# Start addresses of the matmul operands: spare bytes in the slots of the split weights, and a shift of 64 bytes for part of them

## The chip, the cores and the metric

The kernel runs on one core of a Trainium2 chip. The metric is the device time of one execution in microseconds, and smaller is better. Before the change the median of three runs is 1490.11 us (1489.65 to 1490.30). On-chip memory (SBUF) has 128 partitions; a tile of shape `[128, n]` in float32 takes `4 n` bytes at the same byte address in every partition, and "address" below means that byte address. TensorE (PE) multiplies a stationary operand, which a weight load (PEld) puts into the array, with a moving operand, which it streams column by column out of SBUF; the results are added up in PSUM.

## The reference

One layer of a decoder block over 256 tokens of width 2048, in float32: an RMS norm, one wide projection `w_in` (2048 x 11264), three branches (S5 scan, RG-LRU, stick-breaking attention), their gated merge, `w_out`, a residual, a second norm and a squared-ReLU MLP with `w_up` (2048 x 8192) and `w_down` (8192 x 2048), and a last norm.

```
xn = rms_norm(h, norm_mix_g)
proj = xn @ w_in                 # u_s5, u_lru, q, k, v, then 3 x 2048 gate logits
merged = g_s5 * (y_s5 @ w_br_s5) + g_lru * (y_lru @ w_br_lru) + g_attn * (y_attn @ w_br_attn)
h = h + merged @ w_out
hn = rms_norm(h, norm_mlp_g)
h = h + relu(hn @ w_up)**2 @ w_down
return rms_norm(h, final_norm_g)
```

Nearly all the work is in the matrix products with the eight weight matrices.

## The kernel before

**Split operands.** Each float32 matrix product is done as three products of a narrower type (float32r, four bytes in memory): an operand is split into a high part and a low part, and the product is high x high + high x low + low x high.

**The stream of weights.** All weight matrices are cut into units of 256 rows by 512 columns, 128 partitions x 2 x 512 numbers, 4096 bytes a partition. One list, `stream`, orders all 521 units. A unit is loaded into one of three `raw` slots by a DMA from SyncE (L130). ScalarE (ACT) rounds it into a `hi` slot (L146), VectorE (DVE) subtracts to fill a `lo` slot (L147); there are four slots of each, used in turn. `next_unit` keeps four units loaded and three split ahead of TensorE.

**Two forms of a chunk.** A chunk is 512 columns of a weight matrix against all its rows. Both forms compute three matmuls for each piece and differ in what is stationary:

- `chunk` (L225 to L227, tiles `mm_...`), the 256-column form: 128 columns of the weights are stationary, the 256 tokens are moving. The order is: weights `hi` with moving `xhi`, weights `hi` with moving `xlo`, weights `lo` with moving `xhi`. It serves eight chunks of `w_in` (numbers 0 to 7: u_s5, u_lru, q, k) and the two chunks of `w_glu`. There the high and low halves of the moving operand are `xhi`, `xlo` (for `w_glu`: `yg_hi`, `yg_lo`).
- `chunk_tok` (L241 to L243, tiles `mt_...`) and `pair_tok` (L276 to L278, tiles `mp_...`), the 512-column form: 128 tokens are stationary, 512 weight columns are moving. The order is: `xhi` with moving `hi`, `xhi` with moving `lo`, `xlo` with moving `hi`. It serves everything else; the tokens' halves are then `xhi`/`xlo`, `hhi`/`hlo`, or the `yhi`/`ylo` buffers (`ylru_`, `ya_`, `ys_`, `mg_`, `hd_`).

The branches' own work (scans, attention, transposes) is cut into small steps that `pump` issues between units of the stream; their few matmuls (`ps_...`) stand between those of the chunks. They are plain float32, but for `ps_v` (L665), which is float32r with 96 rows. TensorE executes all matmuls in the order in which they are written.

**Which two operands are read at one time.** The weight load of the next matmul is issued while the present matmul streams its moving operand. So in the 256-column form the pairs (moving now, stationary loaded for the next) are `xhi`/`hi`, `xlo`/`lo`, `xhi`/`hi`; in the 512-column form they are `hi`/`xhi`, `lo`/`xlo`, `hi`/`xhi`.

**Where the operands lie.** Pools are laid out one behind the other, and every slice that a matmul reads starts a multiple of 512 bytes into its slot. All sizes of slots are multiples of 512 too, so that in the built program all these slices, `hi`, `lo`, `xhi`, `xlo`, `yhi` and `ylo` alike, start at 32 modulo 512: in both forms, both operands of a pair start at the same address modulo 512. Among the small matmuls' operands, `tri` and `ones` (stationary for `ps_c`), `wrwi`, `stk`, and the attention tiles start at 160 modulo 256, that is 128 further on.

Of the kernel before, what the change touches and what calls it, by code (L numbers as in the profile page):

```python
# [9 lines left out]
F32 = mybir.dt.float32  # L10
F32R = mybir.dt.float32r
# [3 lines left out]
P = 128  # L15
L = 256
D = 2048
KT = D // P
CH = 512
UK = 2  # L20
W = 1024
WT = W // P
NG = 64
NT = 4
# [14 lines left out]
GELU_K = 0.044715  # L39


def units_of(k, n):
    return (n // CH) * (k // (P * UK))

# [2 lines left out]
def hybrid_block(ctx: ExitStack, tc: tile.TileContext, io, out):  # L47
# [2 lines left out]

    const = ctx.enter_context(tc.tile_pool(name="const", bufs=1))
    wraw = ctx.enter_context(tc.tile_pool(name="wraw", bufs=3))
    whi = ctx.enter_context(tc.tile_pool(name="whi", bufs=4))
    act = ctx.enter_context(tc.tile_pool(name="act", bufs=1))
    ypool = ctx.enter_context(tc.tile_pool(name="ypool", bufs=2))
    tmp = ctx.enter_context(tc.tile_pool(name="tmp", bufs=2))
    psm = ctx.enter_context(tc.tile_pool(name="psm", bufs=4, space=PSUM))
    pss = ctx.enter_context(tc.tile_pool(name="pss", bufs=4, space=PSUM))
# [2 lines left out]
    stream = []  # L61
# [36 lines left out]
    for q in range(NQ):  # L98
# [5 lines left out]
        for c in range(2, 4):  # L104
            stream.extend(("w_down", c, q * (FQ // (P * UK)) + g) for g in range(FQ // (P * UK)))
    ngrp = {"w_in": D, "w_br_lru": W, "w_br_attn": W, "w_br_s5": W, "w_glu": W,
            "w_out": D, "w_up": D, "w_down": DFF}

    raw, hi, anchor = {}, {}, {}
    st = {"load": 0, "split": 0, "use": 0}  # L110

    def pieces(i):
        return [slice(k, k + 1) for k in range(UK)] if i == 0 else [slice(0, UK)]
# [19 lines left out]
    def split_next():  # L133
        i = st["split"]
        if i >= len(stream):
            return
        st["split"] += 1
        h = whi.tile([P, UK, CH], F32R, tag="hi", name=f"hi{i}")
        l_ = whi.tile([P, UK, CH], F32R, tag="lo", name=f"lo{i}")
        r = raw.pop(i)  # L140
        x = anchor.pop("x", None)
        es = ExitStack()
        if i == 0:
            es.enter_context(tc.issue_after(x))
        for k in pieces(i):
            anchor["act"] = nc.scalar.copy(h[:, k, :], r[:, k, :]).ins  # L146
            anchor["dve"] = nc.vector.tensor_tensor(l_[:, k, :], r[:, k, :], h[:, k, :].bitcast(F32), ALU.subtract).ins  # L147
        es.close()
        hi[i] = h, l_
# [143 lines left out]

    tc.keep_in_program_order(nc.scalar.preload_act_table_set("natural_log_exp_and_others"))
    gm = small("norm_mix_g")
    xT = act.tile([P, KT, L], F32, tag="m16", name="xT")
    xhi = act.tile([P, KT, L], F32R, tag="xhi", name="xhi")
    xlo = act.tile([P, KT, L], F32R, tag="xlo", name="xlo")
    load_x(0)
    for q in range(3):  # L300
        load_next()
# [30 lines left out]
    nc.gpsimd.affine_select(keep, ones, pattern=[[1, P]], compare_op=ALU.is_gt, fill=0.0, base=0, channel_multiplier=-1)  # L332
    drop = const.tile([P, P], F32, name="drop")
    nc.gpsimd.tensor_scalar(drop, keep, 1e30, -1e30, ALU.mult, ALU.add)
    eps_t = const.tile([P, 1], F32, name="eps_t")
    nc.gpsimd.memset(eps_t, EPS)
    half_pi = const.tile([P, 1], F32, name="half_pi")
    nc.gpsimd.memset(half_pi, math.pi / 2)
    magic = const.tile([P, 1], F32, name="magic")
    nc.gpsimd.memset(magic, MAGIC)  # L340

    def rsqrt_mean(o, ps, n):
# [4 lines left out]
        nc.vector.scalar_tensor_tensor(o, t, 1.5, r, ALU.add, ALU.mult)  # L347

    rstd = const.tile([P, L], F32, name="rstd")
    rstd_tok = const.tile([P, 2], F32, name="rstd_tok")  # L350

    def norm1():
        yield
# [131 lines left out]
    br_ = small("lru_b_r")  # L485
    bi_ = small("lru_b_i")
    lam = small("lru_lambda")
    sp4 = const.tile([P, WT], F32, name="sp4")
    nsp8 = const.tile([P, WT], F32, name="nsp8")
    tiny = const.tile([P, 1], F32, name="tiny")  # L490
    nc.gpsimd.memset(tiny, 2.0 ** -115)
    wrwi = sp.tile([P, 2, WT, P], F32, tag="stk", name="wrwi")
    wr, wi = wrwi[:, 0], wrwi[:, 1]
# [9 lines left out]
    def lru_params():  # L503
        for _ in range(4):
            yield
        lc = const.tile([P, 4, WT], F32, name="lc")
        nc.vector.scalar_tensor_tensor(lc[:, 0, :], lam, -1.0, lam, ALU.mult, ALU.min)
        nc.scalar.activation(lc[:, 1, :], lc[:, 0, :], AF.Exp)
        nc.scalar.activation(lc[:, 2, :], lc[:, 1, :], AF.Ln, bias=1.0)
        nc.vector.tensor_scalar(lc[:, 3, :], lam, -1.0, 0.0, ALU.mult, ALU.max)  # L510
        nc.vector.tensor_tensor(lc[:, 3, :], lc[:, 3, :], lc[:, 2, :], ALU.add)
        nc.vector.tensor_scalar(sp4, lc[:, 3, :], 4.0, None, ALU.mult)
        nc.vector.tensor_scalar(nsp8, lc[:, 3, :], -8.0, None, ALU.mult)
        yield
        yield from lru_load()

    ylru_hi = ypool.tile([P, WT, L], F32R, tag="yhi", name="ylru_hi")
    ylru_lo = ypool.tile([P, WT, L], F32R, tag="ylo", name="ylru_lo")

    def lru_half(c, us):  # L520
        parts = []
# [111 lines left out]
    gq = []  # L633

    def s5_scan():
        v = ypool.tile([P, 2, NT, L], F32, tag="yhi", name="s5_v")
        t12 = ypool.tile([P, 2, NT, L], F32, tag="ylo", name="s5_t")
        vr, vi, t1, t2 = v[:, 0], v[:, 1], t12[:, 0], t12[:, 1]
        tabs, more = s5_tables(0)
        yield from more  # L640
# [18 lines left out]
        for b in range(WT):  # L659
            c, s = tabs  # L660
# [31 lines left out]
            for x_ in (t1, t3):  # L692
                for t in range(NT):
                    j = b * NT + t
# [47 lines left out]
            if n % step == step - 1:  # L742
                yield

    merged = act.tile([P, KT, L], F32, tag="m16", name="merged")
    m_tok = merged.rearrange("p k l -> p (k l)").rearrange("p (t c) -> p t c", t=2)

    def gates(idx, c, alloc):
# [39 lines left out]

    at = ExitStack()
    ap_ = at.enter_context(tc.tile_pool(name="attn", bufs=1))  # L790
    ya_hi = ypool.tile([P, WT, L], F32R, tag="yhi", name="ya_hi")
    ya_lo = ypool.tile([P, WT, L], F32R, tag="ylo", name="ya_lo")
    Z = 384

    def diag(t):
# [84 lines left out]
        finish(t)  # L880


    yg_hi = ypool.tile([P, WT, L], F32R, tag="yhi", name="yg_hi")
    yg_lo = ypool.tile([P, WT, L], F32R, tag="ylo", name="yg_lo")
    for q in range(4):
        s = slice(2 * q, 2 * q + 2)
        nc.scalar.activation(yg_hi[:, s, :], us5[:, s, :], AF.Copy, scale=0.5)
        nc.vector.scalar_tensor_tensor(yg_lo[:, s, :], us5[:, s, :], 0.5, yg_hi[:, s, :].bitcast(F32), ALU.mult, ALU.subtract)
    ys_hi = ypool.tile([P, WT, L], F32R, tag="yhi", name="ys_hi")
    ys_lo = ypool.tile([P, WT, L], F32R, tag="ylo", name="ys_lo")  # L890
    for c in range(2):
        banks = chunk("w_glu", c, W, lambda kt: (yg_hi[:, kt, :], yg_lo[:, kt, :]))
        for j in range(2):
            g = tmp.tile([P, 2, L], F32, tag="gate", name=f"glu_{c}_{j}", bufs=3)
            for h in range(2):
                k = c * 4 + 2 * j + h
# [6 lines left out]
    mg = [None, None]  # L903

    def split_pair(i, n, src):
        if mg[i // 8] is None:
            mg[i // 8] = tuple(ypool.tile([P, WT, L], F32R, tag=t, name=f"mg_{t}{i}") for t in ("yhi", "ylo"))
# [13 lines left out]
    for a in S5_TAIL:  # L921
        c = int(a[1])
# [24 lines left out]
    hT = act.tile([P, KT, L], F32, tag="m16", name="hT")  # L947
    hhi = act.tile([P, KT, L], F32R, tag="xhi", name="hhi")
    hlo = act.tile([P, KT, L], F32R, tag="xlo", name="hlo")
    h_tok = mlp.tile([P, 2, D], F32, name="h_tok")  # L950

    def ms(kt):
# [22 lines left out]
                yield  # L975
        return gen

    rs2 = const.tile([P, 2], F32, name="rs2")
    rq, rfl = [deque(), 2.0, 0.0], {}

    def out_done(c, banks):
# [85 lines left out]
    for q in range(NQ):  # L1067
        hd, hf = {}, {}

        def up_done(cu, banks):  # L1070
            c = cu % (FQ // CH)
            if c % 2 == 0:
                hd[c // 2] = (ypool.tile([P, WT, L], F32R, tag="yhi", name=f"hd_hi{q}_{c}"),
                              ypool.tile([P, WT, L], F32R, tag="ylo", name=f"hd_lo{q}_{c}"))
# [106 lines left out]
```

## Time and profile before

| What | Value |
|---|---|
| Median of three runs | 1490.11 us (1489.65 to 1490.30) |
| The profiled execution's own time | 1491.41 us |
| Its span, first to last instruction | 1489.7 us |
| TensorE busy | 1478.5 us (99%) |
| VectorE busy | 1175.7 us (79%) |
| ScalarE busy | 775.4 us (52%) |
| DMA | 62.5% of 16 engines on the weights' queue |
| Matmuls of the 256-column form | 1728, mean 283 to 287 ns each |
| Matmuls of the 512-column form | 389 ns each |

Matmuls are pipelined: a row's duration runs from a matmul's start to its modelled end, and the next one starts before that. So the pace of TensorE is not in the mean duration but in the distance from one start to the next, which the timeline shows to 0.01 us, and which a count over a window shows more finely. All times in windows are from the start of the span.

### The profile page before, as it was taken

What the parts mean: (1) busy time and instruction counts of PE and PEld (TensorE: products, weight loads), DVE (VectorE), ACT (ScalarE), POOL (GpSimd) and SP (SyncE); (2) the same over time, 40 slices, a digit from 0 to 9 for tenths busy, and PEclk for the clock granted to TensorE, in tenths of its full rate; (3) what the DMA queues carried; (4) which work ended last, traced back from release to release, by engine and by line L of the source; (5) the groups of instructions that cost most, each with busy time, mean ns of one, the idle gap of its engine ahead of it and who ended that gap; (6) DMA issues with size and microseconds to landing.
All of it is one profiled execution on the core that took longest, in us unless ns stands there. A gap on an engine that the chain in (4) does not pass through costs nothing.

```text
span 1489.7 us, 19903 instructions
## 1 busy us (share of the span) xinstructions
PE 1478.5 (99%) x7518; PEld 1259.3 (85%) x7518; DVE 1175.7 (79%) x1470; ACT 775.4 (52%) x915; POOL 48.4 (3%) x73
## 2 busy tenths in 40 slices
PE   9999999999999999999999999999999999999997
PEld 9998888989888888888888888888888888888886
DVE  6878999887989998789799896568754886458955
ACT  6767556565765564544454544344433453344443
POOL 1400000000000000000000000000000000000010
PEclk9999999999999999999999999999999999999999
DMA  9557776655556756566856657666666566666664
GB/s 274 189 157 216 209 229 208 184 165 188 170 177 199 224 184 210 188 187 210 268 183 189 195 184 222 189 193 188 200 194 196 187 197 197 192 190 196 189 198 137
DMA packets 89570, 292.41 MB, mean 196 GB/s; under 512 B 12802, under 2 KB 17026, under 8 KB 89346
## 3 DMA queue, kind: packets, MB, share of 16 engines
q1 hardware_dynamic: 89042, 290.55, 62.5%
q8 instruction: 59, 0.97, 0.3%
q10 hardware_dynamic: 432, 0.59, 0.1%
q14 instruction: 37, 0.30, 0.1%
HBM read 282.71 MB, written 2.10 MB: 191 GB/s over the span
## 4 chain that ended last, share of the span: by engine, by line
PE 95%; DVE 2%; ACT 1%; DMA 1%; issue 1%; DVEq 0%; ACTq 0%; SPq 0%
PE mt_w_in L241 7%; PE mt_w_in L243 7%; PE mt_w_in L242 7%; PE mt_w_up L241 7%; PE mt_w_up L243 7%; PE mt_w_up L242 7%; PE mp_w_down L278 4%; PE mp_w_down L277 4%; PE mp_w_down L276 4%; PE mt_w_down L242 4%; PE mt_w_down L241 4%; PE mt_w_down L243 4%; PE mm_w_in L225 3%; PE mm_w_in L227 3%; PE mm_w_in L226 3%; PE mt_w_br_attn L241 1%
## 5 line engine op out<-in xcount | busy, mean ns | idle before, releaser
L146 ACT CAST hi<-raw 128x1024 fp32r<-128x1024 f32 (+1 forms) x521 | 545.2, 1050 | 614.2 <-PE mt_w_up L243 116.8
L147 DVE TENSOR_TENSOR lo<-raw,hi 128x1024 fp32r<-128x1024 f32 (+1 forms) x521 | 637.1, 1224 | 276.2 <-ACT hi L146 268.5
L241 PE MATMUL mt_w_in<-hi,xhi 128*128 128x512 f32 x448 | 176.2, 393 | 0.0
L243 PE MATMUL mt_w_in<-hi,xlo 128*128 128x512 f32 x448 | 174.5, 389 | 0.0
L242 PE MATMUL mt_w_in<-lo,xhi 128*128 128x512 f32 x448 | 174.4, 389 | 0.0
L241 PE MATMUL mt_w_up<-hi,hhi 128*128 128x512 f32 x448 | 174.3, 389 | 0.0
L242 PE MATMUL mt_w_up<-lo,hhi 128*128 128x512 f32 x448 | 174.3, 389 | 0.0
L243 PE MATMUL mt_w_up<-hi,hlo 128*128 128x512 f32 x448 | 174.3, 389 | 0.0
L225 PE MATMUL mm_w_in<-xhi,hi 128*128 128x256 f32 x512 | 146.7, 287 | 0.7 <-ACT hi L146 0.7
L227 PE MATMUL mm_w_in<-xhi,lo 128*128 128x256 f32 x512 | 145.6, 285 | 1.4 <-DVE lo L147 1.4
L226 PE MATMUL mm_w_in<-xlo,hi 128*128 128x256 f32 x512 | 145.6, 285 | 0.0
L741 DVE STREAM_TRANSPOSE reluT<-relu 32x256 f32<-32x256 f32 x256 | 111.5, 436 | 4.2
L242 PE MATMUL mt_w_down<-lo,hd_hi 128*128 128x512 f32 (+1 forms) x272 | 102.5, 377 | 0.0
L241 PE MATMUL mt_w_down<-hi,hd_hi 128*128 128x512 f32 (+1 forms) x272 | 102.4, 377 | 0.0
L243 PE MATMUL mt_w_down<-hi,hd_lo 128*128 128x512 f32 (+1 forms) x272 | 102.4, 376 | 0.0
L225 PEld LDWEIGHTS mm_w_in<-xhi,hi 128*128 128x128 f32 x512 | 99.1, 194 | 1.9 <-ACT hi L146 1.0
L227 PEld LDWEIGHTS mm_w_in<-xhi,lo 128*128 128x128 f32 x512 | 98.8, 193 | 1.9 <-DVE lo L147 1.8
L276 PE MATMUL mp_w_down<-hi,hd_hi 128*128 128x512 f32 x256 | 99.6, 389 | 0.0
L277 PE MATMUL mp_w_down<-lo,hd_hi 128*128 128x512 f32 x256 | 99.6, 389 | 0.0
L278 PE MATMUL mp_w_down<-hi,hd_lo 128*128 128x512 f32 x256 | 99.6, 389 | 0.0
L226 PEld LDWEIGHTS mm_w_in<-xlo,hi 128*128 128x128 f32 x512 | 99.2, 194 | 0.1
L243 PEld LDWEIGHTS mt_w_in<-hi,xlo 128*128 128x128 f32 x448 | 84.1, 188 | 17.7
(294 smaller groups left out, 2358.1 us busy)
## 6 DMA issues: line engine op xcount, KB each, us to landing
raw<-in_w_in SPq DMA_DIRECT2D x175, 512.0 KB, 4.2
raw<-in_w_up SPq DMA_DIRECT2D x128, 512.0 KB, 4.3
raw<-in_w_down SPq DMA_DIRECT2D x128, 512.0 KB, 4.2
raw<-in_w_out SPq DMA_DIRECT2D x32, 512.0 KB, 4.4
raw<-in_w_br_lru SPq DMA_DIRECT2D x16, 512.0 KB, 4.6
raw<-in_w_br_attn SPq DMA_DIRECT2D x16, 512.0 KB, 4.3
raw<-in_w_br_s SPq DMA_DIRECT2D x16, 512.0 KB, 4.3
stk<-ux SPq DMA_DIRECT2D x96, 64.0 KB, 4.3
```

Source lines behind the costliest of these rows:

```text
L146: anchor["act"] = nc.scalar.copy(h[:, k, :], r[:, k, :]).ins
L147: anchor["dve"] = nc.vector.tensor_tensor(l_[:, k, :], r[:, k, :], h[:, k, :].bitcast(F32), ALU.subtract).ins
L225: nc.tensor.matmul(o, wh[:, kk, s], xh, start=first and ct % 2 == 0, stop=False, skip_group_check=True)
L226: nc.tensor.matmul(o, wh[:, kk, s], xl, start=False, stop=False, skip_group_check=True)
L227: mm = nc.tensor.matmul(o, wl[:, kk, s], xh, start=False, stop=last and ct % 2 == 1, skip_group_check=True)
L241: nc.tensor.matmul(banks[j], xh[:, s], wh[:, a:b], start=kt == 0, stop=False)
L242: nc.tensor.matmul(banks[j], xh[:, s], wl[:, a:b], start=False, stop=False)
L243: return nc.tensor.matmul(banks[j], xl[:, s], wh[:, a:b], start=False, stop=kt == ng * UK - 1)
L276: nc.tensor.matmul(o, xh[:, s], wh[:, kk, :], start=kt == 0, stop=False)
L277: nc.tensor.matmul(o, xh[:, s], wl[:, kk, :], start=False, stop=False)
L278: mm = nc.tensor.matmul(o, xl[:, s], wh[:, kk, :], start=False, stop=kt == ng * UK - 1)
L741: nc.vector.transpose(d_[32 * a:32 * a + 32, :, :, 32 * b:32 * b + 32], s_[32 * b:32 * b + 32, :, :, 32 * a:32 * a + 32])
```

## The change

No instruction is added, removed or moved: on every engine the built program has the same instructions in the same order with the same waits as before. What changes is where tiles lie.

- Each `hi` and `lo` slot is 4160 bytes, 64 more than the unit needs. The slots stand in the order hi0, lo0, hi1, lo1, hi2, lo2, hi3, and lo3 in a pool of its own. Between slots there are 128 bytes of small constants that used to lie in the `const` pool (`lc`, `sp4`, `eps_t` and so on), so that each pair of slots starts 8448 = 33 x 256 bytes after the last.
- The high halves of the tokens (`xhi`, `hhi`, `yhi`) lie in a pool ahead of these slots, the low halves (`xlo`, `hlo`, `ylo`) in one behind them.
- `shift` gives 16 elements, 64 bytes, for units of the 256-column form (`w_glu`, and `w_in` with chunk numbers under 8) and 0 for all others; the split writes the unit that much further into its slot, and the matmuls read it there.

Start addresses in the built programs:

| Operand | Before, modulo 256 | After, modulo 256 |
|---|---|---|
| `xhi`, `hhi`, `yhi` | 32 | 160 |
| `xlo`, `hlo`, `ylo` | 32 | 224 |
| `hi`, 512-column form | 32 | 160 |
| `lo`, 512-column form | 32 | 224 |
| `hi`, 256-column form | 32 | 224 |
| `lo`, 256-column form | 32 | 32 |
| `raw` | 32 | 160 |
| `stk`, `wrwi`, attention tiles, `tri`, `ones` | 160 | 160 |

So the stationary slice of a pair starts, modulo 256, 0 bytes after the moving one in both forms before the change; after it, 0 in the 512-column form and 64 in the 256-column form. Modulo 512 the slots are not alike after the change: `hi` starts at 160 in slots 0 and 2 and at 416 in slots 1 and 3, `lo` at 224 in slots 0 and 2 and at 480 in slots 1 and 3, while the tokens' halves start at 160 and 480.

```diff
+SLOTS = 4
+SHIFT = 16
+
+def shift(name, c, g):
+    return SHIFT if name == "w_glu" or name == "w_in" and c < 8 else 0
...
-    whi = ctx.enter_context(tc.tile_pool(name="whi", bufs=4))
-    act = ctx.enter_context(tc.tile_pool(name="act", bufs=1))
-    ypool = ctx.enter_context(tc.tile_pool(name="ypool", bufs=2))
+    wide = ctx.enter_context(tc.tile_pool(name="wide", bufs=1))
+    act_hi = ctx.enter_context(tc.tile_pool(name="act_hi", bufs=1))
+    wsplit = ctx.enter_context(tc.tile_pool(name="wsplit", bufs=1))
+    act_lo = ctx.enter_context(tc.tile_pool(name="act_lo", bufs=1))
+    wlast = ctx.enter_context(tc.tile_pool(name="wlast", bufs=1))
...
+    def slot(i):
+        j = i % SLOTS
+        pools = wsplit, wlast if j == SLOTS - 1 else wsplit
+        return [p_.tile([P, UK * CH + SHIFT], F32R, tag=f"{n}{j}", name=f"{n}{i}") for p_, n in zip(pools, ("hi", "lo"))]
+
+    def row(name, n):
+        return wsplit.tile([P, n], F32, name=name)
+
+    first = [slot(0)]
+    lc = row("lc", 4 * WT).rearrange("p (a k) -> p a k", a=4)
+    first.append(slot(1))
+    sp4, nsp8, rstd_tok, eps_t = row("sp4", WT), row("nsp8", WT), row("rstd_tok", 2), row("eps_t", 1)
+    first.append(slot(2))
+    half_pi, magic, tiny, rs2 = row("half_pi", 1), row("magic", 1), row("tiny", 1), row("rs2", 2)
+    first.append(slot(3))
...
-        h = whi.tile([P, UK, CH], F32R, tag="hi", name=f"hi{i}")
-        l_ = whi.tile([P, UK, CH], F32R, tag="lo", name=f"lo{i}")
+        o = shift(*stream[i])
+        h, l_ = (t[:, o:o + UK * CH].rearrange("p (k c) -> p k c", k=UK) for t in (first[i] if i < SLOTS else slot(i)))
...
-    xT = act.tile([P, KT, L], F32, tag="m16", name="xT")
-    xhi = act.tile([P, KT, L], F32R, tag="xhi", name="xhi")
-    xlo = act.tile([P, KT, L], F32R, tag="xlo", name="xlo")
+    xT = wide.tile([P, KT, L], F32, tag="m16", name="xT")
+    xhi = act_hi.tile([P, KT, L], F32R, tag="xhi", name="xhi")
+    xlo = act_lo.tile([P, KT, L], F32R, tag="xlo", name="xlo")
...
-    ylru_hi = ypool.tile([P, WT, L], F32R, tag="yhi", name="ylru_hi")
-    ylru_lo = ypool.tile([P, WT, L], F32R, tag="ylo", name="ylru_lo")
+    ylru_hi = act_hi.tile([P, WT, L], F32R, tag="yhi", name="ylru_hi", bufs=2)
+    ylru_lo = act_lo.tile([P, WT, L], F32R, tag="ylo", name="ylru_lo", bufs=2)
```

The other tiles of the old `act` and `ypool` pools move to `wide`, `act_hi` and `act_lo` in the same way.

More of the change, by code (lines that the diff above doesn't have):

```diff
@@ L334, in hybrid_block @@
     nc.gpsimd.tensor_scalar(drop, keep, 1e30, -1e30, ALU.mult, ALU.add)
-    eps_t = const.tile([P, 1], F32, name="eps_t")
     nc.gpsimd.memset(eps_t, EPS)
-    half_pi = const.tile([P, 1], F32, name="half_pi")
     nc.gpsimd.memset(half_pi, math.pi / 2)
-    magic = const.tile([P, 1], F32, name="magic")
     nc.gpsimd.memset(magic, MAGIC)
@@ L349, in hybrid_block @@
     rstd = const.tile([P, L], F32, name="rstd")
-    rstd_tok = const.tile([P, 2], F32, name="rstd_tok")
     def norm1():
@@ L487, in hybrid_block @@
     lam = small("lru_lambda")
-    sp4 = const.tile([P, WT], F32, name="sp4")
-    nsp8 = const.tile([P, WT], F32, name="nsp8")
-    tiny = const.tile([P, 1], F32, name="tiny")
     nc.gpsimd.memset(tiny, 2.0 ** -115)
@@ L505, in lru_params @@
             yield
-        lc = const.tile([P, 4, WT], F32, name="lc")
         nc.vector.scalar_tensor_tensor(lc[:, 0, :], lam, -1.0, lam, ALU.mult, ALU.min)
@@ L635, in s5_scan @@
     def s5_scan():
-        v = ypool.tile([P, 2, NT, L], F32, tag="yhi", name="s5_v")
-        t12 = ypool.tile([P, 2, NT, L], F32, tag="ylo", name="s5_t")
+        v = act_hi.tile([P, 2, NT, L], F32, tag="yhi", name="s5_v", bufs=2)
+        t12 = act_lo.tile([P, 2, NT, L], F32, tag="ylo", name="s5_t", bufs=2)
         vr, vi, t1, t2 = v[:, 0], v[:, 1], t12[:, 0], t12[:, 1]
@@ L743, in blocks @@
                 yield
-    merged = act.tile([P, KT, L], F32, tag="m16", name="merged")
+    merged = wide.tile([P, KT, L], F32, tag="m16", name="merged")
     m_tok = merged.rearrange("p k l -> p (k l)").rearrange("p (t c) -> p t c", t=2)
@@ L790, in hybrid_block @@
     ap_ = at.enter_context(tc.tile_pool(name="attn", bufs=1))
-    ya_hi = ypool.tile([P, WT, L], F32R, tag="yhi", name="ya_hi")
-    ya_lo = ypool.tile([P, WT, L], F32R, tag="ylo", name="ya_lo")
+    ya_hi = act_hi.tile([P, WT, L], F32R, tag="yhi", name="ya_hi", bufs=2)
+    ya_lo = act_lo.tile([P, WT, L], F32R, tag="ylo", name="ya_lo", bufs=2)
     Z = 384
@@ L880, in hybrid_block @@
         finish(t)
-    yg_hi = ypool.tile([P, WT, L], F32R, tag="yhi", name="yg_hi")
-    yg_lo = ypool.tile([P, WT, L], F32R, tag="ylo", name="yg_lo")
+    yg_hi = act_hi.tile([P, WT, L], F32R, tag="yhi", name="yg_hi", bufs=2)
+    yg_lo = act_lo.tile([P, WT, L], F32R, tag="ylo", name="yg_lo", bufs=2)
     for q in range(4):
@@ L888, in hybrid_block @@
         nc.vector.scalar_tensor_tensor(yg_lo[:, s, :], us5[:, s, :], 0.5, yg_hi[:, s, :].bitcast(F32), ALU.mult, ALU.subtract)
-    ys_hi = ypool.tile([P, WT, L], F32R, tag="yhi", name="ys_hi")
-    ys_lo = ypool.tile([P, WT, L], F32R, tag="ylo", name="ys_lo")
+    ys_hi = act_hi.tile([P, WT, L], F32R, tag="yhi", name="ys_hi", bufs=2)
+    ys_lo = act_lo.tile([P, WT, L], F32R, tag="ylo", name="ys_lo", bufs=2)
     for c in range(2):
@@ L906, in split_pair @@
         if mg[i // 8] is None:
-            mg[i // 8] = tuple(ypool.tile([P, WT, L], F32R, tag=t, name=f"mg_{t}{i}") for t in ("yhi", "ylo"))
+            mg[i // 8] = tuple(p_.tile([P, WT, L], F32R, tag=t, name=f"mg_{t}{i}", bufs=2) for p_, t in ((act_hi, "yhi"), (act_lo, "ylo")))
         h_, l_ = mg[i // 8]
@@ L946, in hybrid_block @@
     mf.append(chained(mq, split_tok(3, mlp.tile([P, 4, L], F32, tag="reluT", name="mT3", bufs=2))))
-    hT = act.tile([P, KT, L], F32, tag="m16", name="hT")
-    hhi = act.tile([P, KT, L], F32R, tag="xhi", name="hhi")
-    hlo = act.tile([P, KT, L], F32R, tag="xlo", name="hlo")
+    hT = wide.tile([P, KT, L], F32, tag="m16", name="hT")
+    hhi = act_hi.tile([P, KT, L], F32R, tag="xhi", name="hhi")
+    hlo = act_lo.tile([P, KT, L], F32R, tag="xlo", name="hlo")
     h_tok = mlp.tile([P, 2, D], F32, name="h_tok")
@@ L976, in residual @@
         return gen
-    rs2 = const.tile([P, 2], F32, name="rs2")
     rq, rfl = [deque(), 2.0, 0.0], {}
@@ L1072, in up_done @@
             if c % 2 == 0:
-                hd[c // 2] = (ypool.tile([P, WT, L], F32R, tag="yhi", name=f"hd_hi{q}_{c}"),
-                              ypool.tile([P, WT, L], F32R, tag="ylo", name=f"hd_lo{q}_{c}"))
+                hd[c // 2] = (act_hi.tile([P, WT, L], F32R, tag="yhi", name=f"hd_hi{q}_{c}", bufs=2),
+                              act_lo.tile([P, WT, L], F32R, tag="ylo", name=f"hd_lo{q}_{c}", bufs=2))
             h_, l_ = hd[c // 2]
```

## The prediction

> **What bounds the kernel now.** I read the page's first two parts, then who waits for whom, then TensorE's groups, then single stretches of its timeline.
>
> ```profile
> span 1489.7 us, 19903 instructions
> PE 1478.5 (99%) x7518; PEld 1259.3 (85%) x7518; DVE 1175.7 (79%) x1470; ACT 775.4 (52%) x915; POOL 48.4 (3%) x73
> PE mm_w_in L227 <- DVE lo L147: 1.4, 1, 1.4
> PE warm L327 <- POOL eps_t L336: 1.0, 1, 1.0
> PE mm_w_in L225 <- ACT hi L146: 0.7, 1, 0.7
> ```
>
> The last three rows are all of TensorE's waits: 3.1 us, in the first microseconds. From then on it always has a matmul to start, so the time is the sum of the distances between starts, and a change that moves no instruction can act on it only through these distances, or by making ACT or DVE so late that waits appear. Two groups carry the sum:
>
> ```profile
> L225 PE MATMUL mm_w_in<-xhi,hi 128*128 128x256 f32 x512 | 146.7, 287 | 0.7 <-ACT hi L146 0.7
> L225 PE MATMUL mm_w_glu<-yg_hi,hi 128*128 128x256 f32 x64 | 18.2, 285 | 0.0
> L146 ACT CAST hi<-raw 128x1024 fp32r<-128x1024 f32 (+1 forms) x521 | 545.2, 1050 | 614.2 <-PE mt_w_up L243 116.8
> 587.00:609.00 22.00, 22.00 (x186) 1.00 0.62 193
> 820.00:1460.00 640.00, 640.00 (x2826) 1.00 0.62 195
> ```
>
> The 256-column form has three matmuls of each kind: 3 x (512 + 64) = 1728. Its units are 72 (each gives 24 matmuls); the cast's 521, less one for the first unit, which comes in two pieces, leaves 448 units of 12 matmuls, about 5,380 of the 512-column form. The last two rows are windows with TensorE alone (time, busy, matmuls, granted clock, DMA share, GB/s). Matmuls that only reach into a window at its ends are counted too, about two, so a start comes every 22.0/184 = 0.120 us in the first (256 columns) and every 640/2824 = 0.2266 us in the second (512). The timeline shows the 256-column pace row by row, and the passage to the other form:
>
> ```profile
> 109.43 0.28 PE L225 MATMUL mm_w_in<-xhi,hi 128*128 128x256 f32 x1
> 109.55 0.28 PE L226 MATMUL mm_w_in<-xlo,hi 128*128 128x256 f32 x1
> 109.67 0.28 PE L227 MATMUL mm_w_in<-xhi,lo 128*128 128x256 f32 x1
> ...
> 110.15 0.40 PE L241 MATMUL mt_w_in<-hi,xhi 128*128 128x512 f32 x1
> 110.38 0.40 PE L242 MATMUL mt_w_in<-lo,xhi 128*128 128x512 f32 x1
> 110.61 0.39 PE L243 MATMUL mt_w_in<-hi,xlo 128*128 128x512 f32 x1
> 110.84 0.40 PE L241 MATMUL mt_w_in<-hi,xhi 128*128 128x512 f32 x1
> 111.08 0.39 PE L242 MATMUL mt_w_in<-lo,xhi 128*128 128x512 f32 x1
> 111.31 0.39 PE L243 MATMUL mt_w_in<-hi,xlo 128*128 128x512 f32 x1
> ```
>
> The two paces differ by 226.67 - 120 = 106.67 ns for 256 more columns, 0.4167 ns a column. So 256 columns are 106.67 ns and 512 are 213.33 ns, and **each matmul of either form pays 13.33 ns on top**: 1728 x 13.33 ns = 23 us, and 5,380 x 13.33 ns = 72 us. The question is what this surcharge is made of and whether the start addresses set it.
>
> **Three things the trace says of the surcharge.** First, it is no fixed price of a change of weights:
>
> ```profile
> 9.91 0.41 PE L226 MATMUL mm_w_in<-xlo,hi 128*128 128x256 f32 x1
> 10.13 0.41 PE L227 MATMUL mm_w_in<-xhi,lo 128*128 128x256 f32 x1
> 10.34 0.41 PE L225 MATMUL mm_w_in<-xhi,hi 128*128 128x256 f32 x1
> ...
> 10.73 0.28 PE L227 MATMUL mm_w_in<-xhi,lo 128*128 128x256 f32 x1
> 10.85 0.28 PE L225 MATMUL mm_w_in<-xhi,hi 128*128 128x256 f32 x1
> ...
> 11.91 0.28 PE L226 MATMUL mm_w_in<-xlo,hi 128*128 128x256 f32 x1
> ```
>
> In the first microseconds the same matmuls start every 0.213 us: twice 106.67 ns to within the rounding, with the same weight loads and no surcharge. It is there only when columns are streamed at 0.4167 ns, which is how two readers of one memory would behave: the moving operand, and the weight load of the next matmul beside it.
>
> Second, the surcharge depends on how the two reads stand to each other in time. From 10.73 to 11.91 there are ten matmuls: 118 ns each, below the later 120. After such an unsettled stretch, at the start and behind each side matmul, the pace settles on 120.0 and stays. In the 512-column form it is the other way round: the five from 110.15 to 111.31 take 232 ns each and then settle on 226.67. The settled paces are whole numbers of one step of 6.67 ns, 18 x 6.67 = 120 and 34 x 6.67 = 226.67; 6.67 ns is the time in which 16 columns, 64 bytes, are streamed.
>
> Third, there is one sort of place where the pair's start addresses already differ: where a chunk's matmul streams while a side matmul's weights are loaded, which start 128 bytes further on modulo 256.
>
> ```profile
> 309.72 0.39 PE L241 MATMUL mt_w_in<-hi,xhi 128*128 128x512 f32 x1
> 309.95 0.39 PE L242 MATMUL mt_w_in<-lo,xhi 128*128 128x512 f32 x1
> 310.17 0.40 PE L243 MATMUL mt_w_in<-hi,xlo 128*128 128x512 f32 x1
> 310.41 0.38 PE L819 MATMUL ps_c<-s,tri 128*128 128x256 f32 x1
> ...
> 55.27 0.28 PE L226 MATMUL mm_w_in<-xlo,hi 128*128 128x256 f32 x1
> 55.39 0.28 PE L227 MATMUL mm_w_in<-xhi,lo 128*128 128x256 f32 x1
> 55.51 0.38 PE L540 MATMUL ps_l<-lru_xc,wrwi 128*128 128x256 f32 x1
> ```
>
> The 512-column matmul at 310.17 streams beside the load of `tri`: 0.24 us (at least 0.230) to the next start where 0.2267 is usual, so one step more. The 256-column one at 55.39 streams beside the load of `wrwi`: 0.12 us, no more than usual. So an address difference can cost; what 64 bytes do is in no row.
>
> The Trainium skill, "SBUF — State Buffer", section "SBUF: two separate sides", says that only a port shared by VectorE and GpSimd makes engines wait for each other and that TensorE never waits on anyone there. It would make this change worth nothing, as the second rival does. The rows at 110.15 and 310.17, where the same matmul takes 232 to 240 ns instead of 226.67, do not agree with it as far as TensorE's own two reads go.
>
> **The change part by part.**
>
> The 512-column pairs keep a difference of 0 modulo 256: no cost, about 5,380 x 226.67 ns as before. If it is modulo 512 that counts, half of them no longer have it (third rival).
>
> The 256-column pairs go from 0 to 64 bytes, 1728 of them, less the twenty at the slow pace of the first microseconds and a few behind side matmuls: about 1,700. The settled pace should again be a whole number of steps. Bounds: from below the bare columns, 106.67 ns, a gain of 13.33 ns each or 22.7 us; from above the row at 310.17, one step more, a loss of 11.3 us. Between them I take **one step less, 17 x 6.67 = 113.33 ns**. The reason is the second point above: in this form being out of step was the shorter state (118 against 120), so 120 is neither a floor of the weight load nor of the columns, and the difference of 0 locks this form into its longer state; a shift by one step's worth of bytes takes it from there. That not both steps go is my guess from the unsettled matmuls, none of which comes near 106.67. So 1,700 x -6.67 ns = -11.3 us.
>
> The side pairs like 243/`tri` go from 128 to 0 modulo 256: about 30 places at one step each, -0.2 us.
>
> ACT and DVE write to other addresses. I cost that at nothing: TensorE waits for them for 2.1 us in all. The cover is thinnest where the S5 scan runs:
>
> ```profile
> 200.00:600.00 400.00, 400.00 (x2310) 347.18 (x2309) 358.11 (x405) 239.03 (x297) 8.77 (x10) 1.00 0.63 194
> ```
>
> DVE (the third pair of numbers after the time) is busy for 358 of 400 us, so 42 us are spare; if its subtraction, 1.2 us a unit, took a tenth longer, about 150 units there would cost 18 us of it, and still nothing.
>
> DMAs, slots and waits are the same in number and order. Sum: -11.3 - 0.2 = -11.5 us. The profiled execution took 1491.41 us with 1489.7 in its span, 1.3 us over the median; it would take 1479.9, and the median 1490.1 - 11.5 = **1478.6 us**.
>
> **The rivals.**
>
> 1. *Slower: the 64 bytes cost a step instead of saving one.* Place: every 256-column pair. Price 6.67 ns x 1,700 = 11.3 us, 1501.4 us; it decides as soon as the settled pace is above 120. For it: the one differing pair in the 512-column form costs a step. Against: the same difference in the 256-column form does not. 13%.
> 2. *Nothing changes.* The pace settles on 18 steps whatever the start addresses, because what settles it is time and not place: 1490.0 us. For it: the row at 55.39, the nearest to the new case, at 0.12 us; and slices at every multiple of 512 bytes give the same pace. 21%.
> 3. *Slower in the 512-column form, by modulo 512.* Half of its pairs differ by 256 now; at the price of the row at 310.17 that is 2,690 x 6.67 ns = 18 us, 1496.5 us with the forecast's gain beside it and 1508 without. Against: this form's tokens start at every multiple of 512 alone, so no row shows it either way. 10%.
> 4. *The pace does not settle* and stays between 117 and 118.5 ns as from 10.73 to 11.91: -2.5 to -5 us, 1485 to 1487.6 us. 10%.
> 5. *Nearly all of the surcharge goes*, 107 to 110 ns: -17 to -22 us, 1468 to 1473 us. 8%. For what remains when reads do not meet, the Trainium skill ("TensorE: Matmul & The Clock Gate", section "Wait — 56ns, not 53.3ns?") gives 2.5 ns a matmul; by it the estimate would be 109.2 ns and 1471.5 us. No run here shows it.
>
> **How the numbers follow.** The forecast has 38%, with 1477 to 1480 us as its own range. A measurement of this kernel can tell about 0.2%, 3 us, from no change. Faster is the forecast with rivals 4 and 5: 56%. Same is rival 2: 21%. Slower are rivals 1 and 3: 23%. The range reaches from within rival 5 to just over rival 1, 1470 to 1502 us, and leaves out the far ends of rivals 3 and 5, under 10%.
>
> **What would show it.** Step by step: in the window of `w_glu` the count of starts per microsecond gives 113.3 ns (forecast), 120 (rival 2), 126.7 (rival 1), or a pace that is no whole number of steps (rival 4). In the `w_up` and `w_down` stretch the pace is 226.67 ns unless rival 3 holds, and then it differs between even and odd slots. The passage from the 256- to the 512-column form and the matmul ahead of `ps_c` should change too, the latter to 0.227 us. The forecast is wrong as a whole if TensorE has waits for `hi` or `lo` beyond the first microseconds, since then the time no longer is the sum of its paces.

## The result, and the profile after

| | Before | Changed |
|---|---|---|
| Median of four runs each, taken side by side | 1490.2 us (1489.65 to 1492.59) | 1511.88 us (1511.33 to 1512.74) |
| The profiled execution's own time | 1491.41 us | 1511.43 us |
| Its span | 1489.7 us | 1509.7 us |

The changed kernel takes 1.0143 times as long, with a 95% interval of 1.0125 to 1.016. It is slower by 21.7 us; 11.5 us less were forecast.

The changed kernel's page (span, engines, then four of TensorE's groups):

```profile
span 1509.7 us, 19903 instructions
PE 1497.8 (99%) x7518; PEld 1256.2 (83%) x7518; DVE 1176.4 (78%) x1470; ACT 774.6 (51%) x915; POOL 47.0 (3%) x73
...
L267 PE MATMUL mt_w_up<-hi,hhi 128*128 128x512 f32 x448 | 177.0, 395 | 0.0
L268 PE MATMUL mt_w_up<-lo,hhi 128*128 128x512 f32 x448 | 176.5, 394 | 0.0
L269 PE MATMUL mt_w_up<-hi,hlo 128*128 128x512 f32 x448 | 175.2, 391 | 0.0
L251 PE MATMUL mm_w_in<-xhi,hi 128*128 128x256 f32 x512 | 145.9, 285 | 0.6 <-ACT hi L172 0.6
```

Its table of who waits for whom, all of TensorE's rows:

```profile
PE mm_w_in L253 <- DVE lo L173: 2.0, 2, 1.5
PE warm L353 <- POOL eps_t L361: 1.0, 1, 1.0
PE mm_w_in L251 <- ACT hi L172: 0.6, 2, 0.4
```

ACT and DVE are as busy as before, and TensorE waits for 3.6 us where it waited for 3.1. So the time is still the sum of the distances between TensorE's starts, and these have grown. L267 to L269 are the lines L241 to L243 of before: the 512-column form, whose groups went from 389 ns each to 391 to 395. L251 was L225: the 256-column form, slightly shorter, 285 where it was 287. **The time came in where nothing was expected.** The timeline in the middle of `w_up` shows it:

```profile
999.92 0.40 PE L267 MATMUL mt_w_up<-hi,hhi 128*128 128x512 f32 x1
1000.15 0.39 PE L268 MATMUL mt_w_up<-lo,hhi 128*128 128x512 f32 x1
1000.38 0.39 PE L269 MATMUL mt_w_up<-hi,hlo 128*128 128x512 f32 x1
1000.61 0.40 PE L267 MATMUL mt_w_up<-hi,hhi 128*128 128x512 f32 x1
...
1002.69 0.40 PE L267 MATMUL mt_w_up<-hi,hhi 128*128 128x512 f32 x1
```

From the first row to the last are four times three matmuls in 2.77 us: 693 ns for three, which is 104 steps of 6.67 ns, where before three took 102 (680 ns). In the finer start times of the trace the three distances are 232.5, 231.7 and 229.2 ns on average over `w_up` and `w_down`, in the order of the lines, and they repeat. In `w_up` all four slots show the same three distances, even and odd ones alike.

Two windows of the changed kernel, for TensorE alone (time, busy, matmuls, granted clock, DMA share, GB/s), the first in `w_glu` with 256 columns, the second in `w_up` and `w_down` with 512:

```profile
592.00:608.00 16.00, 16.00 (x137) 1.00 0.59 180
840.00:1440.00 600.00, 600.00 (x2598) 1.00 0.60 190
```

The second window in the kernel before:

```profile
840.00:1440.00 600.00, 600.00 (x2649) 1.00 0.62 195
```

With two matmuls off for the ends, as in the prediction, a start comes every 16/135 = 0.1185 us (it was 0.120) and every 600/2596 = 0.2311 us (it was 600/2647 = 0.2267). The granted clock is 1.00 as before. The sums over the whole trace, from the means between undisturbed starts:

| Form | Before | Changed | Matmuls | Difference |
|---|---|---|---|---|
| 512 columns | 226.84 ns | 231.29 ns | 5,380 | +23.9 us |
| 256 columns | 119.96 ns | 118.51 ns | 1,700 | -2.5 us |

The sum is +21.5 us before rounding, and the medians differ by 21.7 us.

### The profile page after: what moved, and what is told of

It is laid out like the page before. It is cut to its first block, busy times and chain, and to the rows that moved or that the text cites. A ratio compares the mean times of both kernels' runs of the same rounds, so it can differ in the third digit from the quotient of the medians.

```text
span 1509.7 us, 19903 instructions
## 1 busy us (share of the span) xinstructions
PE 1497.8 (99%) x7518; PEld 1256.2 (83%) x7518; DVE 1176.4 (78%) x1470; ACT 774.6 (51%) x915; POOL 47.0 (3%) x73
## 4 chain that ended last, share of the span: by engine, by line
PE 93%; DVE 2%; DMA 2%; ACT 1%; issue 1%; POOL 0%; SPq 0%; DVEq 0%; ACTq 0%
PE mt_w_in L267 7%; PE mt_w_up L267 7%; PE mt_w_up L268 7%; PE mt_w_in L268 7%; PE mt_w_in L269 7%; PE mt_w_up L269 7%; PE mp_w_down L302 4%; PE mp_w_down L303 4%; PE mp_w_down L304 4%; PE mt_w_down L267 4%; PE mt_w_down L268 4%; PE mt_w_down L269 4%; PE mm_w_in L251 2%; PE mm_w_in L253 2%; PE mm_w_in L252 2%; DMA raw<-in_w_in 2%
## 5 line engine op out<-in xcount | busy, mean ns | idle before, releaser
L267 PE MATMUL mt_w_in<-hi,xhi 128*128 128x512 f32 x448 | 178.3, 398 | 0.0
L267 PE MATMUL mt_w_up<-hi,hhi 128*128 128x512 f32 x448 | 177.0, 395 | 0.0
L269 PE MATMUL mt_w_in<-hi,xlo 128*128 128x512 f32 x448 | 175.8, 392 | 0.0
L269 PE MATMUL mt_w_up<-hi,hlo 128*128 128x512 f32 x448 | 175.2, 391 | 0.0
L251 PE MATMUL mm_w_in<-xhi,hi 128*128 128x256 f32 x512 | 145.9, 285 | 0.6 <-ACT hi L172 0.6
L267 PE MATMUL mt_w_down<-hi,hd_hi 128*128 128x512 f32 (+1 forms) x272 | 103.8, 381 | 0.0
L269 PE MATMUL mt_w_down<-hi,hd_lo 128*128 128x512 f32 (+1 forms) x272 | 102.8, 378 | 0.0
L269 PEld LDWEIGHTS mt_w_up<-hi,hlo 128*128 128x128 f32 x448 | 84.2, 188 | 20.1
L269 PEld LDWEIGHTS mt_w_in<-hi,xlo 128*128 128x128 f32 x448 | 84.2, 188 | 19.8
L267 PEld LDWEIGHTS mt_w_up<-hi,hhi 128*128 128x128 f32 x448 | 84.2, 188 | 19.6
L267 PEld LDWEIGHTS mt_w_in<-hi,xhi 128*128 128x128 f32 x448 | 84.3, 188 | 19.1 <-issue 0.8
```

Of the source, the lines that this page charges most:

```text
L251: nc.tensor.matmul(o, wh[:, kk, s], xh, start=first and ct % 2 == 0, stop=False, skip_group_check=True)
L267: nc.tensor.matmul(banks[j], xh[:, s], wh[:, a:b], start=kt == 0, stop=False)
L269: return nc.tensor.matmul(banks[j], xl[:, s], wh[:, a:b], start=False, stop=kt == ng * UK - 1)
```

## The experiments

The question is what in the addresses lengthened the 512-column form, although each of its pairs still starts at the same address modulo 256, and why the 256-column form gained 1.45 ns and not 6.67. The change does two things to addresses, and they can be done apart:

- **Own residues.** High and low halves no longer start alike: each has a residue (its start modulo 256) of its own. So the start jumps from one matmul to the next: the moving start goes 160, 224, 160 modulo 256 in the 512-column form, and the stationary one 160, 160, 224.
- **The shift.** In the 256-column form the weights start 64 bytes further on than the tokens.

The expectations speak of four theories. A: the jumps break the settled pace. B, the prediction's own: only the difference within a pair counts. C: moving start, stationary start and their difference all count, with equal starts fast in the 512-column form and slow in the 256-column form. D: only the jumps cost anything, and a constant difference is harmless. C and D were set up after the results of the first four of the runs below (no shift, `lo` alone, the tokens' low halves alone, all weights by 64 bytes).

In all texts below, "the weights lie 64 bytes further on" is meant against the tokens, modulo 256. Weights are stationary in the 256-column form and moving in the 512-column form.

### Own residues without the shift

```diff
 def shift(name, c, g):
-    return SHIFT if name == "w_glu" or name == "w_in" and c < 8 else 0
+    return 0
```

> The changed kernel with the shift of 64 bytes set to 0 for all units; the spare bytes and the places of the pools stay. Every pair (moving now, stationary loaded for the next) then starts at the same address modulo 256, as before the change, but high parts start at 160 and low parts at 224. Theory A (the settled pace needs successive matmuls whose operands start at the same residue; own residues for high and low parts break it, whatever the pair's difference): 512-column triple of matmuls near the 693.3 ns of the changed kernel instead of 680, 256-column form off its 120 ns too, about 1510 us. Theory B (the pair's difference sets the pace): 226.7 and 120 ns, 1490 us.

Measured: 1510.17 us (two runs), 1.012 times the kernel before (1.009 to 1.0149). The window of `w_up` and `w_down`:

```profile
840.00:1440.00 600.00, 600.00 (x2598) 1.00 0.61 190
```

It has the same count as the changed kernel, and over the whole trace the 512-column form takes 231.09 ns. Every pair of both forms has a difference of 0 here, as before the change. So the difference within a pair is not all that counts, and B falls. **The loss belongs to the own residues.** The 256-column form takes 117.79 ns here without any shift. So in the changed kernel the gain of the 256-column form came from the residues, not from the shift, which on top of them made it 118.51.

### One jump at a time

The pools are put in an order that lets each operand be moved alone, with unused bytes between them:

```diff
-    whi = ctx.enter_context(tc.tile_pool(name="whi", bufs=4))
-    act = ctx.enter_context(tc.tile_pool(name="act", bufs=1))
-    ypool = ctx.enter_context(tc.tile_pool(name="ypool", bufs=2))
+    wide = ...          # m16: xT, merged, hT
+    pad("pad0", 0)
+    act_hi = ...        # xhi, hhi, yhi
+    pad("pad1", 0)
+    whi = ...           # hi
+    pad("pad2", 64)
+    wlo = ...           # lo
+    pad("pad3", 192)
+    act_lo = ...        # xlo, hlo, ylo
+    pad("pad4", 0)
```

This is the kernel in which only `lo` lies 64 bytes further on.

> The kernel before, with pools put in another order and 64 bytes left free ahead of the lo slots alone: hi, xhi, xlo, yhi, ylo start at 32 modulo 256, lo at 96. In the 512-column form only the moving operand jumps from matmul to matmul (hi, lo, hi), in the 256-column form only the stationary one. Theory A, moving operand: 512-column triple about 693 ns, 256-column form 120 ns each, about 1513 us. Theory A, stationary operand: 512-column form 226.7 ns, 256-column form off 120 ns, 1484 to 1490 us. Theory B (pairs hi/xhi 0, lo/xlo -64): the 512-column form changes by a third of its matmuls at most.

In the other, only the low halves of the tokens do:

```diff
-    pad("pad2", 64)
+    pad("pad2", 0)
-    pad("pad3", 192)
+    pad("pad3", 64)
-    pad("pad4", 0)
+    pad("pad4", 192)
```

> The kernel before, with pools in another order and 64 bytes left free ahead of the low halves of the tokens alone: xlo, hlo, ylo start at 96 modulo 256, hi, lo and the high halves at 32. In the 256-column form only the moving operand jumps, in the 512-column form only the stationary one. Theory A, moving operand: 512-column form 226.7 ns, 256-column form about 118.5 ns, 1487 us. Theory A, stationary operand: 512-column triple about 693 ns, 256-column form 120 ns, about 1513 us.

Measured: with `lo` moved 1515.55 us (two runs; 1.0156 times, 1.0126 to 1.0185), with the tokens' low halves moved 1511.05 us (two runs; 1.0125 times, 1.0096 to 1.0155). The same window, of the kernel with `lo` moved:

```profile
840.00:1440.00 600.00, 600.00 (x2588) 1.00 0.60 189
```

and of the kernel with the tokens' low halves moved:

```profile
840.00:1440.00 600.00, 600.00 (x2598) 1.00 0.61 190
```

That is 600/2586 = 232.0 and 600/2596 = 231.1 ns. In the 512-column form the first makes only the moving start jump, the second only the stationary one. **Either move alone is enough**, and both together, with the pairs back at a difference of 0, cost no more. Each of the two also gives one pair in three a difference, so by themselves they do not tell a jump from a difference; the next kernels show what a difference costs alone.

### A constant difference without jumps

Here all halves of the weights, high and low, are moved by the same amount, so that no start jumps within a form, and all pairs have the same difference. Only the unused bytes change, against those above:

```diff
+    pad("pad1", 64)     # 128, 192, 32 in the other three
+    pad("pad2", 0)
+    pad("pad3", 192)    # 128, 64, 224 in the other three
```

> The kernel before, with pools in another order and 64 bytes left free ahead of both hi and lo: all weights start at 96 modulo 256, all tokens' halves at 32. No operand jumps between residues from one matmul to the next; every pair differs by 64 bytes, in the 256-column form in the same direction as after the change. Theory A: 120 and 226.7 ns, 1490 us. Theory B as in the prediction: the 256-column form settles one step lower or higher (113.3 or 126.7 ns, -11 or +11 us) and the 512-column form changes too.

> As the run with all weights 64 bytes on, but 128: hi and lo start 128 bytes after the tokens' halves modulo 256, and no operand jumps from one matmul to the next. Theory C (three relations count, the pair's difference, the jump of the moving and the jump of the stationary operand; equal starts everywhere are the fast case of the 512-column form and the slow case of the 256-column form): the 512-column form near the 233 ns that a matmul beside the load of tri takes, 256-column form 116 to 120 ns, about 1515 us. Theory D (only the jumps cost in the 512-column form, and the 2 ns that the 64-byte run lost there are a state that had not settled): 226.7 ns and 1484 to 1490 us.

> All weights start 192 bytes after the tokens' halves modulo 256, that is 64 before them; no operand jumps. Theory C, if the sign of the difference does not count: as the run with 64 bytes, 229 and 116.3 ns, about 1497 us; if the sign counts, another pair of paces, between 226.7 and 235 ns for 512 columns. Theory D: 226.7 ns.

> All weights start 32 bytes after the tokens' halves modulo 256; no operand jumps. If differences count in blocks of 64 bytes that begin at multiples of 64, the weights (at 64) and the tokens (at 32) lie in different blocks, and the paces are near those of the 64-byte run (229 and 116 ns, 1497 us); if the difference counts by bytes, about half of its effect (227.8 and 118 ns, 1493 us).

Measured: at 64 bytes 1496.87 us (five runs; 1.0033 times, 1.0017 to 1.0049). The others have one run each beside one of the kernel before at 1490.74 us: 1517.38 us at 128 bytes, 1519.66 us at 192 and 1525.84 us at 32. The window with 512 columns, of the kernel with 64 bytes:

```profile
840.00:1440.00 600.00, 600.00 (x2623) 1.00 0.61 192
```

of that with 128:

```profile
840.00:1440.00 600.00, 600.00 (x2583) 1.00 0.60 188
```

of that with 192:

```profile
840.00:1440.00 600.00, 600.00 (x2574) 1.00 0.60 188
```

and of that with 32:

```profile
840.00:1440.00 600.00, 600.00 (x2573) 1.00 0.60 188
```

That is 228.9, 232.5, 233.3 and 233.3 ns for 512 columns, the last two being 35 steps. A constant difference costs too, so D falls: at 64 bytes 2 ns a matmul, at the others 5.6 to 6.5. The sign counts, for 192 bytes forward are 64 bytes back and cost three times as much as 64 forward. The size does not order the losses: 32 bytes cost as much as 192, and both expectations for that kernel (229 and 227.8 ns) failed.

With these numbers the two kernels with one jump can be read. With only `lo` moved, one pair of three has the difference of the kernel with 64 bytes; a third of that kernel's loss is 0.7 ns, and the form loses 5.2. With only the tokens' low halves moved, one pair of three has the difference of the kernel with 192 bytes; a third of its loss is 2.2 ns, and the form loses 4.3. So if the pairs' costs simply add up, which no run shows, each jump has a cost of its own; the first experiment showed without any difference that the two jumps together have one.

The 256-column form gains from each of the four: 116.26 ns at 64 bytes, 118.66 at 128, 117.30 at 192 and 118.33 at 32, against 119.96. In the kernel with 64 bytes, the window in `w_glu` has the forecast's pace:

```profile
587.00:603.00 16.00, 16.00 (x143) 1.00 0.63 191
```

16/141 = 0.1135 us, 17 steps. The mean of 116.26 ns comes about because `w_in` does not have this pace everywhere: in the finer start times of the trace it takes 113.3 ns from 14 to 39 us and 117.8 ns from 249 to 291 us. In the kernel with 192 bytes `w_glu` takes 113.3 ns, too, and `w_in` 117.8.

### All operands together

In the same order of pools everything is moved by 32 bytes, and no difference and no jump arises:

```diff
+    pad("pad0", 32)
+    pad("pad1", 0)
+    pad("pad2", 0)
+    pad("pad3", 0)
+    pad("pad4", 224)
```

> The kernel before with hi, lo and all halves of the tokens moved on by 32 bytes, so that all start at 64 modulo 256 instead of 32; all differences and jumps stay 0. If only relations between the operands count (theories C and D): 120 and 226.7 ns, 1490 us. If the place in a 64-byte block counts (a slice that starts in the middle of a block touches one block more): up to one step of 6.67 ns less for each matmul, down to 113.3 and 220 ns, 1443 us.

Measured: 1490.56 us (one run; the kernel before beside it 1490.74).

```profile
840.00:1440.00 600.00, 600.00 (x2648) 1.00 0.62 194
```

That is 600/2646 = 226.8 ns, and the 256-column form takes 119.94. Where all starts lie together, inside a block of 64 bytes or at its edge, makes no difference, and neither does the new order of the pools. As far as these two places show, only how the starts lie to each other counts.

### The shift without own residues

If equal starts are best for 512 columns and worst for 256, the shift should be made without the residues. The order of pools is as above with no unused bytes between; each slot of the weights gets 256 spare bytes, and only units of the 256-column form are written 64 bytes further into it. To make room, the attention's `s` has two buffers and not three.

```diff
+SPARE = 64
+SHIFT = 16          # elements: 64 bytes; 4, 24, 56 in the other three
...
+        o = shift(*stream[i])
-        h = whi.tile([P, UK, CH], F32R, tag="hi", name=f"hi{i}")
-        l_ = whi.tile([P, UK, CH], F32R, tag="lo", name=f"lo{i}")
+        h = whi.tile([P, UK * CH + SPARE], F32R, tag="hi", name=f"hi{i}")
+        l_ = wlo.tile([P, UK * CH + SPARE], F32R, tag="lo", name=f"lo{i}")
+        h, l_ = (t[:, o:o + UK * CH].rearrange("p (k c) -> p k c", k=UK) for t in (h, l_))
...
-            s_ = ap_.tile([P, Z], F32, tag="s", name=f"s{h}", bufs=3)
+            s_ = ap_.tile([P, Z], F32, tag="s", name=f"s{h}", bufs=2)
```

> The shift without own residues: all operands at 32 modulo 256 as before, slots 256 bytes longer, and only the units of the 256-column form 64 bytes further on (hi and lo alike). To make room the attention's s buffers are two instead of three, which moves a few small instructions there. Theory C (each form has the pace that its own pairs had in the uniform runs): 512-column form 226.7 ns as before, 256-column form 116.3 ns as in the run with all weights 64 bytes on; 3.7 ns x 1,700 = 6.3 us less than before, 1484 us, ratio 0.9958. The prediction's step (17 steps, 113.3 ns): 1479 us. If the shift as such is harmful: 1490 us or more.

> As the run before it, but the units of the 256-column form lie 16 bytes further on. Theory C: 512-column form 226.7 ns; the 256-column pace somewhere between the 120.0 ns of 0 bytes and the 118.3 ns that 32 bytes gave, 1487 to 1490 us.

> As the run before it, with 96 bytes. Theory C: 512-column form 226.7 ns; the 256-column pace between the 116.3 ns of 64 bytes and the 118.7 ns of 128, 1484 to 1488 us.

> As the run before it, with 224 bytes, that is 32 before the tokens' start modulo 256. Theory C: 512-column form 226.7 ns; the 256-column pace between the 117.3 ns of 192 bytes and the 120.0 ns of 0, 1486 to 1490 us.

Measured: with 64 bytes 1487.92 us (ten runs, the kernel before beside them 1490.39 in thirteen; 0.9984 times, 0.9974 to 0.9993). **It is faster than both kernels, if by little.** One run each of the others: 1488.83 us with 16 bytes, 1488.86 with 96, 1487.56 with 224. No run has two buffers for `s` without the shift, so what these cost by themselves is not shown. The two windows of the kernel with 64 bytes:

```profile
587.00:603.00 16.00, 16.00 (x143) 1.00 0.63 196
840.00:1440.00 600.00, 600.00 (x2649) 1.00 0.62 194
```

The 512-column form keeps its 226.7 ns, and `w_glu` has 17 steps. By its size, 4352 bytes, every other slot starts 256 bytes further on modulo 512 against the tokens here, as in the changed kernel. All four slots show 226.7 ns in `w_up`, so modulo 512 has no part in the loss. But over the whole trace the 256-column form takes 115.61 ns, not 113.33, because it settles in two ways. Two stretches of the timeline of this kernel:

```profile
59.77 0.28 PE L246 MATMUL mm_w_in<-xhi,hi 128*128 128x256 f32 x1
60.12 0.28 PE L246 MATMUL mm_w_in<-xhi,hi 128*128 128x256 f32 x1
60.45 0.28 PE L246 MATMUL mm_w_in<-xhi,hi 128*128 128x256 f32 x1
60.80 0.28 PE L246 MATMUL mm_w_in<-xhi,hi 128*128 128x256 f32 x1
...
329.76 0.28 PE L246 MATMUL mm_w_in<-xhi,hi 128*128 128x256 f32 x1
330.11 0.28 PE L246 MATMUL mm_w_in<-xhi,hi 128*128 128x256 f32 x1
330.46 0.28 PE L246 MATMUL mm_w_in<-xhi,hi 128*128 128x256 f32 x1
330.82 0.28 PE L246 MATMUL mm_w_in<-xhi,hi 128*128 128x256 f32 x1
```

From one L246 to the next there are three matmuls. Near 60 us nine take 1.02 us in the finer start times of the trace, 51 steps for each three, so 113.3 ns a matmul. Near 330 us nine take 1.06 us, 53 steps for each three, so 117.8 ns. The form, the lines and the start addresses modulo 256 are the same in both. A stretch keeps its pace, but for the first one or two threes, until a distance of 140 ns or more interrupts it (mostly a side matmul or a wait), and may go on with the other pace behind it. `w_in` has the longer pace without a break from 248.1 to 290.3 and from 324.8 to 360.4 us; then `ps_v` stands in between, and from 361.3 to 363.6 us it has the shorter. Before 100 us it has mostly the shorter, and in `w_glu` that alone.

Part of the gain is given back, and TensorE's waits show one place:

```profile
PE mm_w_in L248 <- DVE lo L168: 3.5, 4, 2.3
PE warm L348 <- POOL eps_t L357: 1.0, 1, 1.0
PE mm_w_in L246 <- ACT hi L167: 0.7, 1, 0.7
PE ps_n L387 <- DVE xT L383: 0.2, 1, 0.2
```

It waits for 5.4 us and not 3.1, above all for DVE's `lo`. By their pace the 256-column matmuls should shorten the trace by 7.4 us. The span is shorter by 4.5 us. The rest lies in the distances of 140 ns and more behind a 256-column matmul, mostly those with a wait or a side matmul in them. In this kernel there are 44, 13.8 us in all, and in the kernel before 35, 9.5 us; nine more at the usual pace would be only 1.1 us of that.

Theory C's pace for 512 columns came in all four kernels. For 256 columns its 116.3 ns at 64 bytes were near, and the paces with 16 and 96 bytes lie within the bounds expected; that with 224 bytes, 116.81 ns, lies under them. The times with 64 and 96 bytes lie above those expected.

### All kernels in one table

The sum is worked out as for the changed kernel: the two differences of pace to 226.84 and 119.96 ns, times 5,380 and 1,700. The time is the difference to the kernel before that ran beside it.

| Kernel | 512 columns, ns | 256 columns, ns | Sum, us | Time, us |
|---|---|---|---|---|
| Changed kernel | 231.29 | 118.51 | +21.5 | +21.7 |
| Own residues, no shift | 231.09 | 117.79 | +19.2 | +19.0 |
| Only `lo` +64 | 231.99 | 117.86 | +24.1 | +24.4 |
| Only tokens' low halves +64 | 231.10 | 119.46 | +22.1 | +19.9 |
| Weights +64 | 228.99 | 116.26 | +5.3 | +5.7 |
| Weights +128 | 232.47 | 118.66 | +28.1 | +26.6 |
| Weights +192 | 233.31 | 117.30 | +30.3 | +28.9 |
| Weights +32 | 233.31 | 118.33 | +32.0 | +35.1 |
| All +32 | 226.95 | 119.94 | +0.6 | -0.2 |
| 256-column units +64 | 226.84 | 115.61 | -7.4 | -2.5 |
| 256-column units +16 | 226.87 | 118.34 | -2.6 | -1.6 |
| 256-column units +96 | 226.86 | 118.00 | -3.2 | -1.5 |
| 256-column units +224 | 226.83 | 116.81 | -5.4 | -2.8 |

The two paces account for the losses to within about 3 us. For the 256-column units at +64 the sum of -7.4 us leaves out the long distances; the span, which has them, is 4.5 us shorter. But the profiled execution, 1486.94 us, was the shortest of its ten, that of the kernel before, 1491.41 us, is above its median, and by the medians 2.5 us are left.

## Why the prediction was wrong

**What bounds the kernel** held. TensorE has no new wait of weight in the changed kernel, and its time is the sum of its paces.

**"The 512-column pairs keep a difference of 0 modulo 256: no cost" is the step that failed.** It took the two reads of a pair for the whole relation. The pairs did keep their difference of 0, and the form lost 4.45 ns on each of about 5,380 matmuls. The kernel with own residues and no shift shows the cause: all pairs at 0 and 231.09 ns. What was lost is the second thing that the old layout had, one start for high and low halves, so that no start jumped from one matmul to the next. The prediction had read that 226.67 ns is a settled pace, which the form loses behind side matmuls and finds again; it did not ask what else, besides the pair, must repeat for it to settle. Of the 5,380 and the 1,700 matmuls the first were the dearer risk by three to one, and the term set at nothing was the one that needed bounds. By the row at 310.17, which stood in the prediction, one step on all of them would have been 5,380 x 6.67 ns = 36 us; the layouts tried reach from 0 to nearly that, 6.47 ns or 35 us.

**"The 256-column pairs go from 0 to 64 bytes ... one step less"** had the right sign and the wrong size: 1.45 ns in place of 6.67, 2.5 us in place of 11.3. In this kernel the sign is luck: the own residues alone give 117.79 ns, and the shift on top of them lengthens that to 118.51. The state of 17 steps exists, in `w_glu` with 64 bytes and no jumps. With the own residues the form does not reach it: its distances repeat over nine matmuls, 160 steps, 118.5 ns. Without them the form takes 113.3 ns in some stretches and 117.8 in others, so that even there the term would have been 4.35 x 1,700 = 7.4 us.

**That ACT and DVE's new addresses cost nothing** held: 3.6 us of waits against 3.1, and the same busy times. **The side pairs' 0.2 us** came out at about half ahead of `ps_c`, as the timeline of the changed kernel shows:

```profile
310.34 0.39 PE L269 MATMUL mt_w_in<-hi,xlo 128*128 128x512 f32 x1
310.57 0.59 PE L837 MATMUL ps_c<-s,tri 128*128 128x256 f32 x2
```

In the finer start times the matmul that streams beside the load of `tri` takes 230 ns to the next start in all eight such places, where it took 233 to 234. The 227 ns forecast did not come; L269 now takes 229 ns ahead of any other matmul.

**The rivals.** The first (a step more in the 256-column form) and the second (nothing changes) are refuted by 118.51 ns. The third named the right place, the 512-column form, and nearly the right time, 1508 us, by a mechanism that did not occur: modulo 512 should have told even slots from odd ones, and both show the same distances, in the changed kernel and in the one with the 256-column units 64 bytes on. The fourth gave 117 to 118.5 ns for the 256-column form, and 118.51 came, but not as a pace that does not settle: the distances repeat every nine matmuls. It said nothing of the other form. The fifth (107 to 110 ns) is not borne out: no kernel's settled pace lies under 113.33 ns. The range ended at 1502 us because no case let the 512-column form lose in all its pairs.

On the Trainium skill's rule in "SBUF — State Buffer", section "SBUF: two separate sides", that TensorE never waits on anyone there: between the kernel before and the one with own residues and no shift, only addresses differ, and a matmul of 512 columns goes from 226.84 to 231.09 ns. As far as TensorE's own reads are concerned, these runs do not agree with it.

**What stays open.** Why a jump of the start costs, and why 512 columns are best at equal starts and 256 columns worst there, is not shown; that two reads of one memory meet is the picture that led to the experiments, and no row shows such a meeting. Nor is it shown what decides, behind an interruption, whether a stretch of the 256-column form settles at 113.3 or at 117.8 ns. The kernel with the weights 32 bytes further on is 6 us slower than that with 192 at the same 512-column pace; 1.7 us of it are its 256-column pace and 2.0 us its waits (5.6 us against 3.6); the rest is not accounted for, and each of the two has one run.

## What to carry to other kernels

When a kernel is bound by the distance between TensorE's starts, its layout in memory is a setting like any other: count starts over a window of each form, turn the difference to the bare columns into time for all matmuls of that form, and give the form with the most matmuls the first look. Keep equal what a settled pace may rest on, the starts of high and low halves as well as those of a pair, and change one relation at a time, in the form where it gains. A layout edit that "keeps" a relation for the larger form still needs a bound for what else it moves there.

## What the runs showed of the hardware that was not expected

- Start addresses alone, with the same instructions in the same order, move a 512-column matmul with its weight load between 226.8 and 233.3 ns and a 256-column one between 113.3 and 120 ns.
- The two forms answer in opposite ways: equal starts without jumps give 512 columns their shortest pace of those tried (226.8 ns; 228.99 to 233.31 at a constant difference) and 256 columns their longest (119.96 ns; 115.61 to 118.66 at a constant difference).
- Settled paces are whole numbers of 6.67 ns over a cycle and not always over one matmul: 104 steps for three matmuls of 512 columns in the changed kernel, 160 for nine of 256 columns, 53 for three of 256 columns at 64 bytes.
- At the same start addresses modulo 256 there are two such states of the 256-column form, 113.3 and 117.8 ns. Each is held until a distance of 140 ns or more interrupts it, the longer one for over a hundred threes in a row from 248 to 290 us.
- Moving all operands by 32 bytes together changes neither pace (226.95 and 119.94 ns), and a difference of 256 bytes in every other slot does not change that of 512 columns (226.84 ns).
